# Rotary embedding: larger units, a smaller sine table spread by TensorE, and stores moved between queues

## The chip, the cores and the metric

The kernel runs on one core of a Trainium2 chip. The metric is the device time of one execution in microseconds (us). Seven executions of the kernel before had a median of 85.37 us, from 85.22 to 85.55. The profile comes from one execution and shows five engines (TensorE as PE, VectorE as DVE, ScalarE as ACT, GpSimd as POOL, SyncE as SP) and the 16 DMA engines, which carry the transfers of all queues.

## The reference

The input x has 8 batches of 8 heads, 1024 positions and 64 columns in float32, 16.8 MB. Each position is scaled by 0.5 and multiplied with 32 frequencies; the two halves of the 64 columns are then rotated by that angle.

```python
half = x.shape[-1] // 2
angles = np.outer(positions * scale, freqs)          # 1024 x 32
cos, sin = np.cos(angles), np.sin(angles)
x_first, x_second = x[..., :half], x[..., half:]
out_first = x_first * cos - x_second * sin
out_second = x_first * sin + x_second * cos
out = np.concatenate([out_first, out_second], axis=-1)
```

All 64 heads use the same table of 1024 x 32 sines and cosines. The output is as large as the input.

## The kernel before

The 64 heads are cut into 8 units of 8 heads (L40 to L44). A unit is 2 MB of float32; partition p holds 64 successive positions of one head, so its row is 4096 numbers, 16 KB in memory, and every unit needs the same table of 64 positions x 32 frequencies per partition, because the 16 partitions of a head repeat for each of the 8 heads.

**Loads.** Unit 0 comes in as float32 through SyncE's queue into X0f (L61) and is cast to fp16 by ScalarE (L127). Units 1 to 7 are loaded by GpSimd (L71), whose transfers cast from float32 to fp16 on the way. Each unit has a tile of its own, X0 to X7, so no load waits for anything, and all seven are issued in the first microseconds. Positions and frequencies come in through ScalarE's queue (L64, L66), in this order.

**Table.** The positions lie on 16 partitions, 64 to each. A matmul with a selecting matrix of zeros and ones (sel, made on GpSimd at L76 and L77) repeats them on all 128 partitions (pos_ps, L100). A second one multiplies the frequencies by scale/2pi on every partition (cfreq, L92). VectorE forms the product y (L107), rounds it (m, L114), takes the remainder r (L116) and its absolute value ra (L122), all for 128 x 2048. ScalarE turns r into sinT (L120) and ra into cosT (L126), both fp16.

**Units.** A loop in the order 1, 0, 2, ... 7 (L133) does four VectorE instructions for a unit: ps = X sin (L135), X = X cos (L136), the first half less the product of the second (L137), and the sum for the second half (L140). ScalarE casts the result to float32 into OUT (L144), and SyncE stores it (L145). OUT has 4 buffers, ps has 2.

**Order.** The kernel's author fixes the order on VectorE and ScalarE by hand: `pin` keeps instructions in the order of the program on their engine. Between the engines only the data sets the order: a load ahead of its unit, a cast ahead of its store, and a free buffer ahead of a cast into OUT.

Of the kernel before, what the change touches and what calls it, by code (L numbers as in the profile page):

```python
# [1 line left out]

# [1 line left out]

# [4 lines left out]

FP32 = mybir.dt.float32
FP16 = mybir.dt.float16
I32 = mybir.dt.int32
AF = mybir.ActivationFunctionType
ALU = mybir.AluOpType

_MAGIC = 12582912.0
_TWO_PI_DN = float(np.float32(np.uint32(0x40C90FDA).view(np.float32)))

BUF_O = 4  # L20
BUF_P = 2


@with_exitstack
def kernel(
    ctx: ExitStack,
    tc: tile.TileContext,
    x: bass.AP,
    freqs: bass.AP,
    positions: bass.AP,  # L30
    scale: bass.AP,
    out: bass.AP,
):
    nc = tc.nc

    B, Hh, S, D = x.shape
    NBH = B * Hh
    half = D // 2
    P = nc.NUM_PARTITIONS
    HEADS = 8  # L40
    HP = P // HEADS
    K = S // HP
    N = K * D
    NU = NBH // HEADS  # L44
    assert S % HP == 0 and D == 2 * half and NBH % HEADS == 0

    fscale = float(scale)

    xv = x.rearrange("b h s d -> (b h s d)").rearrange("(u p n) -> u p n", p=P, n=N)
    ov = out.rearrange("b h s d -> (b h s d)").rearrange("(u p n) -> u p n", p=P, n=N)  # L50

    consts = ctx.enter_context(tc.tile_pool(name="consts", bufs=1))
    tmp = ctx.enter_context(tc.tile_pool(name="tmp", bufs=1))
    psum = ctx.enter_context(tc.tile_pool(name="psum", bufs=1, space=bass.MemoryType.PSUM))
    xin = ctx.enter_context(tc.tile_pool(name="xin", bufs=1))
    xout = ctx.enter_context(tc.tile_pool(name="xout", bufs=BUF_O))
    prods = ctx.enter_context(tc.tile_pool(name="prods", bufs=BUF_P))


    X0f = xin.tile([P, N], FP32, name="X0f")  # L60
    nc.sync.dma_start(out=X0f, in_=xv[0])  # L61

    pos_i64 = consts.tile([HP, K], positions.dtype)
    nc.scalar.dma_start(out=pos_i64, in_=positions.rearrange("(q k) -> q k", k=K))  # L64
    freq_row = consts.tile([1, half], FP32)
    nc.scalar.dma_start(out=freq_row, in_=freqs[None, :])  # L66

    X = [xin.tile([P, K, 2, half], FP16, name=f"X{u}") for u in range(NU)]

    def load(u):  # L70
        nc.gpsimd.dma_start(out=X[u].rearrange("p k h j -> p (k h j)"), in_=xv[u])  # L71


    sel = consts.tile([HP, HEADS, HP], FP32)
    load(1)
    nc.gpsimd.memset(sel, 0.0)  # L76
    nc.gpsimd.affine_select(  # L77
        out=sel, in_=sel, compare_op=ALU.not_equal, fill=1.0, base=0,
        pattern=[[0, HEADS], [-1, HP]], channel_multiplier=1,
    )  # L80
    for u in range(2, NU):
        load(u)

    pin = tc.keep_in_program_order


    coef = consts.tile([1, P], FP32)
    pin(nc.vector.memset(coef, fscale / (2.0 * np.pi)))  # L88
    quarter = consts.tile([P, 1], FP32)
    pin(nc.vector.memset(quarter, np.pi / 2.0))  # L90
    cfreq = psum.tile([P, half], FP32)
    nc.tensor.matmul(out=cfreq, lhsT=coef, rhs=freq_row, start=True, stop=True)  # L92

    pos_row = consts.tile([HP, K], FP32)
    pin(nc.vector.tensor_copy(  # L95
        out=pos_row,
        in_=pos_i64.bitcast(I32).rearrange("p (k t) -> p k t", t=2)[:, :, 0],
    ))
    pos_ps = psum.tile([P, K], FP32)
    nc.tensor.matmul(  # L100
        out=pos_ps, lhsT=sel.rearrange("q a b -> q (a b)"), rhs=pos_row, start=True, stop=True
    )
    posf = consts.tile([P, K], FP32)
    pin(nc.vector.tensor_copy(out=posf, in_=pos_ps))  # L104

    y = tmp.tile([P, K, half], FP32)
    pin(nc.vector.tensor_tensor(  # L107
        out=y,
        in0=posf.unsqueeze(2).broadcast_to((P, K, half)),
        in1=cfreq.unsqueeze(1).broadcast_to((P, K, half)),  # L110
        op=ALU.mult,
    ))
    m = tmp.tile([P, K, half], FP32)
    pin(nc.vector.tensor_scalar(out=m, in0=y, scalar1=_MAGIC, scalar2=None, op0=ALU.add))  # L114
    r = tmp.tile([P, K, half], FP32)
    pin(nc.vector.scalar_tensor_tensor(  # L116
        out=r, in0=m, scalar=_MAGIC, in1=y, op0=ALU.subtract, op1=ALU.subtract
    ))
    sinT = consts.tile([P, K, half], FP16)
    pin(nc.scalar.activation(out=sinT, in_=r, func=AF.Sin, bias=0.0, scale=-_TWO_PI_DN))  # L120
    ra = tmp.tile([P, K, half], FP32)
    pin(nc.vector.tensor_scalar(  # L122
        out=ra.bitcast(I32), in0=r.bitcast(I32), scalar1=0x7FFFFFFF, scalar2=None, op0=ALU.bitwise_and
    ))
    cosT = consts.tile([P, K, half], FP16)
    pin(nc.scalar.activation(out=cosT, in_=ra, func=AF.Sin, bias=quarter, scale=-_TWO_PI_DN))  # L126
    pin(nc.scalar.copy(out=X[0].rearrange("p k h j -> p (k h j)"), in_=X0f))  # L127

    cos_b = cosT.unsqueeze(2).broadcast_to((P, K, 2, half))
    sin_b = sinT.unsqueeze(2).broadcast_to((P, K, 2, half))  # L130


    for u in (1, 0, *range(2, NU)):  # L133
        ps = prods.tile([P, K, 2, half], FP16, tag="ps")
        pin(nc.vector.tensor_tensor(out=ps, in0=X[u], in1=sin_b, op=ALU.mult))  # L135
        pin(nc.vector.tensor_tensor(out=X[u], in0=X[u], in1=cos_b, op=ALU.mult))  # L136
        pin(nc.vector.tensor_tensor(  # L137
            out=X[u][:, :, 0, :], in0=X[u][:, :, 0, :], in1=ps[:, :, 1, :], op=ALU.subtract
        ))
        pin(nc.vector.tensor_tensor(  # L140
            out=X[u][:, :, 1, :], in0=ps[:, :, 0, :], in1=X[u][:, :, 1, :], op=ALU.add
        ))
        OUT = xout.tile([P, N], FP32, tag="O")
        pin(nc.scalar.copy(out=OUT, in_=X[u].rearrange("p k h j -> p (k h j)")))  # L144
        nc.sync.dma_start(out=ov[u], in_=OUT)  # L145


# [1 line left out]
_INS = ['x', 'freqs', 'positions', 'scale']  # L149
_OUTS = [((8, 8, 1024, 64), 'float32')]  # L150

_NUMBERS = {'scale': 0.5}


# [26 lines left out]
```

## Time and profile before

| What | Value |
|---|---|
| median of 7 executions | 85.37 us (85.22 to 85.55) |
| the profiled execution | 85.22 us, its span 83.4 us |
| VectorE busy | 62.6 us, 75% of the span, 40 instructions |
| ScalarE busy | 37.4 us, 45%, 12 instructions |
| GpSimd busy | 4.5 us; TensorE 1.1 us |
| HBM read and written | 16.79 and 16.78 MB |

The span runs from the first to the last event that the profile holds; the time of an execution is some 1.8 us longer. The profile gives the busy share of each engine in 40 slices of 2.1 us, with digits for tenths; the shares of the DMA queues, where q1 is SyncE's, q10 ScalarE's and q0 GpSimd's; the chain of work that ended last; and groups of like instructions by line, with their count, busy time, mean duration and the idle time of the engine ahead of them. A window gives, for a stretch of the span, its length, then busy time and count for PE, PE's weight loads, VectorE, ScalarE and GpSimd, then the TensorE clock granted, the DMA share, and the GB/s that arrived. The trace also holds each packet of each DMA queue with its start, duration and size.

### The profile page before, as it was taken

What the parts mean: (1) busy time and instruction counts of PE and PEld (TensorE: products, weight loads), DVE (VectorE), ACT (ScalarE), POOL (GpSimd) and SP (SyncE); (2) the same over time, 40 slices, a digit from 0 to 9 for tenths busy, and PEclk for the clock granted to TensorE, in tenths of its full rate; (3) what the DMA queues carried; (4) which work ended last, traced back from release to release, by engine and by line L of the source; (5) the groups of instructions that cost most, each with busy time, mean ns of one, the idle gap of its engine ahead of it and who ended that gap; (6) DMA issues with size and microseconds to landing.
All of it is one profiled execution on the core that took longest, in us unless ns stands there. A gap on an engine that the chain in (4) does not pass through costs nothing.

```text
span 83.4 us, 151 instructions
## 1 busy us (share of the span) xinstructions
PE 1.1 (1%) x4; PEld 0.9 (1%) x4; DVE 62.6 (75%) x40; ACT 37.4 (45%) x12; POOL 4.5 (5%) x13
## 2 busy tenths in 40 slices
PE   0003100000000000000000000000000000000000
PEld 0004000000000000000000000000000000000000
DVE  0010899699999999999999999999999999600000
ACT  1400000899559129509806912940970691394000
POOL 5960000000000000000000000000000000000000
DMA  5699999999999998999999999999999999999890
GB/s 110 240 342 349 279 200 232 208 224 204 220 220 200 232 177 243 377 302 338 287 318 369 291 330 298 357 463 401 463 408 440 432 416 463 393 471 393 377 503 0
DMA packets 2338, 26.22 MB, mean 314 GB/s; under 512 B 274, under 2 KB 290, under 8 KB 290
## 3 DMA queue, kind: packets, MB, share of 16 engines
q1 hardware_dynamic: 1296, 18.87, 54.2%
q0 software_dynamic: 1008, 7.34, 42.9%
q10 hardware_dynamic: 34, 0.01, 0.1%
HBM read 16.79 MB, written 16.78 MB: 402 GB/s over the span
## 4 chain that ended last, share of the span: by engine, by line
DVE 72%; DMA 7%; ACT 7%; DVEq 1%; PE 1%; issue 1%; ACTq 1%
DVE X L136 22%; DVE ps L135 21%; DVE X L137 12%; DVE X L140 10%; DMA freq_row<-in_freqs_dram 7%; ACT OUT L144 4%; DVE r L116 3%; DVE y L107 3%; ACT sinT L120 2%; DVE m L114 1%; DVEq L176 1%; PE cfreq L92 1%; PE pos_ps L100 1%; ACTq L64 0%; DVE posf L104 0%
## 5 line engine op out<-in xcount | busy, mean ns | idle before, releaser
L144 ACT CAST OUT<-X 128x4096 f32<-128x4096 f16 x8 | 28.8, 3605 | 25.0 <-DVE X L140 25.0
L135 DVE TENSOR_TENSOR ps<-X,sinT 128x4096 f16<-128x4096 f16 x8 | 18.3, 2285 | 0.7 <-ACT sinT L120 0.7
L136 DVE TENSOR_TENSOR X<-X,cosT 128x4096 f16<-128x4096 f16 x8 | 18.3, 2292 | 0.3
L137 DVE TENSOR_TENSOR X<-X,ps 128x2048 f16<-128x2048 f16 x8 | 9.8, 1225 | 0.3
L140 DVE TENSOR_TENSOR X<-ps,X 128x2048 f16<-128x2048 f16 x8 | 9.7, 1217 | 0.0
L120 ACT ACTIVATE sinT<-r 128x2048 f16<-128x2048 f32 x1 | 1.9, 1910 | 11.8 <-DVE r L116 11.8
L71 POOL DMA_DIRECT2D X<-in_x_dram x7 | 3.9, 567 | 0.8 <-POOLq L162 0.8
L127 ACT CAST X<-X0f 128x4096 f16<-128x4096 f32 x1 | 3.6, 3588 | 0.0
L95 DVE CAST pos_row<-pos_i 16x64 f32<-16x64 int32 x1 | 0.3, 272 | 3.8 <-DMA pos_i<-in_positions_dram 3.8
L104 DVE COPY posf<-pos_ps 128x64 f32<-128x64 f32 x1 | 0.2, 225 | 3.5 <-PE pos_ps L100 3.5
L116 DVE SCALAR_TENSOR_TENSOR r<-m,y 128x2048 f32<-128x2048 f32 x1 | 2.3, 2293 | 0.0
L107 DVE TENSOR_TENSOR y<-posf,cfreq 128x2048 f32<-128x2048 f32 x1 | 2.3, 2287 | 0.0
L120 ACT ACT_TABLE_LOAD x1 | 1.3, 1283 | 1.7 <-issue 1.7
L126 ACT ACTIVATE cosT<-ra,quarter 128x2048 f16<-128x2048 f32 x1 | 2.0, 1985 | 0.0
L114 DVE TENSOR_SCALAR m<-y 128x2048 f32<-128x2048 f32 x1 | 1.2, 1226 | 0.0
L122 DVE TENSOR_SCALAR ra<-r 128x2048 int32<-128x2048 int32 x1 | 1.2, 1226 | 0.0
L88 DVE MEMSET coef<- 1x128 f32 x1 | 0.2, 165 | 0.8 <-PEq L162 0.8
L92 PE MATMUL cfreq<-freq_row,coef 1*128 1x32 f32 x2 | 0.6, 391 | 7.5 <-DMA freq_row<-in_freqs_dram 7.5
L100 PE MATMUL pos_ps<-pos_row,sel 16*128 16x64 f32 x2 | 0.7, 432 | 0.0
L92 PEld LDWEIGHTS cfreq<-freq_row,coef 1*128 1x128 f32 x2 | 0.5, 304 | 7.5 <-issue 7.5
L100 PEld LDWEIGHTS pos_ps<-pos_row,sel 16*128 16x128 f32 x2 | 0.5, 328 | 0.0
L77 POOL TENSOR_SCALAR_AFFINE_SELECT sel<-sel 16x128 f32<-16x128 f32 x1 | 0.3, 333 | 0.1
(6 smaller groups left out, 0.7 us busy)
## 6 DMA issues: line engine op xcount, KB each, us to landing
out_dram<-OUT SPq DMA_DIRECT2D x8, 2048.0 KB, 14.5
X<-in_x_dram POOLq DMA_DIRECT2D x7, 1024.0 KB, 24.4
X0f<-in_x_dram SPq DMA_DIRECT2D x1, 2048.0 KB, 10.2
pos_i<-in_positions_dram ACTq DMA_DIRECT2D x1, 8.0 KB, 4.1
freq_row<-in_freqs_dram ACTq DMA_DIRECT2D x1, 0.1 KB
```

What stands on the lines that cost most here:

```text
L71: nc.gpsimd.dma_start(out=X[u].rearrange("p k h j -> p (k h j)"), in_=xv[u])
L100: nc.tensor.matmul(out=pos_ps, lhsT=sel.rearrange("q a b -> q (a b)"), rhs=pos_row, start=True, stop=True)
L107: pin(nc.vector.tensor_tensor(out=y, in0=posf.unsqueeze(2).broadcast_to((P, K, half)), in1=cfreq.unsqueeze(1).broadcast_to((P, K, half)), ...
L114: pin(nc.vector.tensor_scalar(out=m, in0=y, scalar1=_MAGIC, scalar2=None, op0=ALU.add))
L116: pin(nc.vector.scalar_tensor_tensor(out=r, in0=m, scalar=_MAGIC, in1=y, op0=ALU.subtract, op1=ALU.subtract))
L120: pin(nc.scalar.activation(out=sinT, in_=r, func=AF.Sin, bias=0.0, scale=-_TWO_PI_DN))
L127: pin(nc.scalar.copy(out=X[0].rearrange("p k h j -> p (k h j)"), in_=X0f))
L135: pin(nc.vector.tensor_tensor(out=ps, in0=X[u], in1=sin_b, op=ALU.mult))
L136: pin(nc.vector.tensor_tensor(out=X[u], in0=X[u], in1=cos_b, op=ALU.mult))
L137: pin(nc.vector.tensor_tensor(out=X[u][:, :, 0, :], in0=X[u][:, :, 0, :], in1=ps[:, :, 1, :], op=ALU.subtract))
L140: pin(nc.vector.tensor_tensor(out=X[u][:, :, 1, :], in0=ps[:, :, 0, :], in1=X[u][:, :, 1, :], op=ALU.add))
L144: pin(nc.scalar.copy(out=OUT, in_=X[u].rearrange("p k h j -> p (k h j)")))
```

## The change

The units become twice as large: 4 units of 16 heads, 4 MB each. Partition p holds 128 successive positions of a head, so the row of a unit is 8192 numbers, 32 KB in memory. The computation of a unit is done in two halves of 4096 numbers per partition, with the same four VectorE instructions and one ScalarE cast for each half as before for a unit. The loop runs in the order 0 to 3.

Loads: the second half of unit 0 comes in as float32 in two quarters, one through SyncE and one through ScalarE, the latter behind positions and frequencies; the two land in a buffer of OUT's pool. GpSimd loads the first half of unit 0 and the whole of units 1 to 3. On GpSimd, the memset and the select that make sel are now pinned between its loads, and sel has 128 x 2048 elements in fp16 instead of 16 x 128 in float32.

Table: the positions come in on 128 partitions, 8 to each, so that y, m, r, ra and the two Sin instructions have 256 columns. Their results lie in one tile tab. Sixteen fp16 matmuls of 512 columns, each with another slice of sel, copy the rows of tab to where the units need them; six PSUM buffers take the results. Groups 0, 2, 4 and 6 are copied from PSUM into the table T by VectorE, the other twelve by ScalarE, which then casts the second half of unit 0.

Stores: units 0 and 1 are stored whole by GpSimd, after its loads; units 2 and 3 by SyncE, half by half. OUT has 3 buffers of 32 KB per partition, one of which first holds unit 0's two quarters.

```diff
-    HEADS = 8
+    HEADS = 16
...
-    X0f = xin.tile([P, N], FP32, name="X0f")
-    nc.sync.dma_start(out=X0f, in_=xv[0])
-    pos_i64 = consts.tile([HP, K], positions.dtype)
-    nc.scalar.dma_start(out=pos_i64, in_=positions.rearrange("(q k) -> q k", k=K))
+    X0f = xout.tile([P, N], FP32, tag="O")
+    Q = NH // 2
+    pin(nc.sync.dma_start(out=X0f[:, :Q], in_=xv[0][:, NH : NH + Q]))
+    pos_i64 = consts.tile([P, K8], positions.dtype)
+    pin(nc.scalar.dma_start(out=pos_i64, in_=positions.rearrange("(p k) -> p k", k=K8)))
     freq_row = consts.tile([1, half], FP32)
-    nc.scalar.dma_start(out=freq_row, in_=freqs[None, :])
+    pin(nc.scalar.dma_start(out=freq_row, in_=freqs[None, :]))
+    pin(nc.scalar.dma_start(out=X0f[:, Q:NH], in_=xv[0][:, NH + Q :]))
...
+    sel = consts.tile([P, G, HEADS, HP], FP16)
+    pin(nc.gpsimd.dma_start(out=Xf[0][:, :NH], in_=xv[0][:, :NH]))
+    pin(nc.gpsimd.memset(sel, 0.0))
+    pin(nc.gpsimd.dma_start(out=Xf[1], in_=xv[1]))
+    pin(nc.gpsimd.affine_select(
         out=sel, in_=sel, compare_op=ALU.not_equal, fill=1.0, base=0,
-        pattern=[[0, HEADS], [-1, HP]], channel_multiplier=1,
-    )
+        pattern=[[-1, G], [0, HEADS], [-G, HP]], channel_multiplier=1,
+    ))
     for u in range(2, NU):
-        load(u)
+        pin(nc.gpsimd.dma_start(out=Xf[u], in_=xv[u]))
...
+    T = consts.tile([P, 2, K, half], FP16)
+    for g in range(G):
+        ps = spread.tile([P, 2, K8, half], FP32, tag="g")
+        nc.tensor.matmul(
+            out=ps.rearrange("p t k j -> p (t k j)"),
+            lhsT=sel[:, g].rearrange("s h q -> s (h q)"),
+            rhs=tab.rearrange("s t k j -> s (t k j)"),
+            start=True, stop=True,
+        )
+        dst = T[:, :, g * K8 : (g + 1) * K8, :]
+        if g % 2 == 0 and g < G // 2:
+            pin(nc.vector.tensor_copy(out=dst, in_=ps))
+        else:
+            pin(nc.scalar.copy(out=dst, in_=ps))
+    pin(nc.scalar.copy(out=Xf[0][:, NH:], in_=X0f[:, :NH]))
...
-    for u in (1, 0, *range(2, NU)):
+    for u in range(NU):
+        OUT = xout.tile([P, N], FP32, tag="O")
+        for s in range(2):
+            ks = slice(s * KH, (s + 1) * KH)
+            ns = slice(s * NH, (s + 1) * NH)
...
+            pin(nc.scalar.copy(out=OUT[:, ns], in_=Xf[u][:, ns]))
+            if u >= NU // 2:
+                pin(nc.sync.dma_start(out=ov[u][:, ns], in_=OUT[:, ns]))
+        if u < NU // 2:
+            pin(nc.gpsimd.dma_start(out=ov[u], in_=OUT))
```

Here KH is half of K (64), NH half of N (4096), K8 is 8 positions per partition, and G is 16 groups.

## The prediction

> **What bounds the kernel now.** I read the slices of the page first, then its queues, then windows of 5 us.
>
> ```profile
> DVE  0010899699999999999999999999999999600000
> ...
> DMA  5699999999999998999999999999999999999890
> ...
> q1 hardware_dynamic: 1296, 18.87, 54.2%
> q0 software_dynamic: 1008, 7.34, 42.9%
> ...
> HBM read 16.79 MB, written 16.78 MB: 402 GB/s over the span
> ```
>
> ```profile
> 10.00:15.00 5.00, 0.00 (x0) 0.00 (x0) 4.90 (x4) 0.19 (x1) 0.00 (x0) 1.00 1.03 215
> 40.00:45.00 5.00, 0.00 (x0) 0.00 (x0) 4.97 (x4) 1.68 (x2) 0.00 (x0) 1.00 1.01 316
> 60.00:65.00 5.00, 0.00 (x0) 0.00 (x0) 4.93 (x4) 2.14 (x1) 0.00 (x0) 1.00 0.99 423
> ```
>
> The DMA share is the seventh number of the windows, after the clock, and it is 1.0 in all three stages: loads alone, loads and stores mixed, stores alone. The GB/s beside it count what arrives: a load turns float32 into fp16, so 215 arriving is 430 read, 316 is half of each, and 423 is stores. The transfers thus run at one rate from end to end, and the two queues' shares sum to 97.1% of 83.4 us. VectorE is as long a job: the chain that ended last is nearly all VectorE.
>
> ```profile
> 1.19 6.21 DMA freq_row<-in_freqs_dram
> ...
> 7.53 0.60 PE cfreq L92 x2
> ...
> 14.81 1.92 ACT sinT L120
> 16.75 2.30 DVE ps L135
> ...
> 71.16 1.15 DVEq L176
> ...
> 72.38 3.60 ACT OUT L144
> ```
>
> freqs lands at 7.40, the tables take 9.35 us more, and 8 units of 6.94 us run from 16.75 to 72.31. The cast of the last unit ends at 75.98. In the trace's packet records the last store's first row starts at 76.85, just as the one before it drains (77.0); its last row ends at 81.9, its completion is there at 82.27, and 1.18 us of ending follow. So **two bounds meet at the end**: the transfers have no gap to give back, and VectorE has none to lose. A gain must make the transfers shorter, and keep VectorE from becoming later.
>
> **The change, transfers.** No byte is saved; the rows are. The packet records give for a row of 16 KB 625 ns on GpSimd's queue (q0), 611 ns for a store alone on q1 (624 beside loads), and 22 and 9 ns for a bare completion of 4 B. A straight line through row and completion puts a row of 32 KB at 1.228 us on q0, 22 ns under two of 16 KB, and one of 8 KB at 0.315. For each of the 16 DMA engines:
> - before: 56 x 0.625 + 8 x 0.62 (X0f) + 28 x 0.624 + 36 x 0.611 + 0.24 of completions = 79.7 us. From the first packet (1.76) to the last row it took 80.16, so 0.46 go to the cold start and to the first store's arrival.
> - after: loads 16 x 0.315 + 8 x 0.625 + 24 x 1.228 = 39.5; stores 16 x 1.228 (q0) + 32 x 0.611 (SyncE's halves) = 39.2; completions and the small rows of positions 0.45; sum 79.2.
>
> That is **-0.5 us**. No row of 32 KB is in the trace. If it costs as much as two, the 40 of them give 0.9 back (+0.4); if the 0.46 vanish because loads and stores no longer mix until the loads are over, it is -1.0. I take -0.5.
>
> **The change, VectorE's start.** Positions now lie 8 to a partition, so the angles are 256 columns instead of 2048. Two lengths of one kind give the fixed part: VectorE 2285 ns at 4096 and 1220 at 2048, so 155 fixed; ScalarE 3605 at 4096 and 1910 at 2048, so 214.
>
> ```profile
> L144 ACT CAST OUT<-X 128x4096 f32<-128x4096 f16 x8 | 28.8, 3605 | 25.0 <-DVE X L140 25.0
> ...
> L107 DVE TENSOR_TENSOR y<-posf,cfreq 128x2048 f32<-128x2048 f32 x1 | 2.3, 2287 | 0.0
> ```
>
> Count from F, the landing of freqs (7.40 before). cfreq with its issue 0.74; y 0.42; m 0.29; r 0.42; gaps 0.1; sin 0.43; cos 0.5: cos ends at F+2.9. The pos_ps matmul and its copy fall away, and ra lies beside sin. Then 16 selecting matmuls of 512 columns and 16 copies out of PSUM. No such matmul is in the trace: L92 (32 columns, float32) took 391 ns and L100 (64) 432, so 0.39 to 1.0 us. The Trainium skill (TensorE: Matmul & The Clock Gate, Back-to-back issue gap) has columns/1.2 ns while the array is cold, 0.43 each, near the lower end, and I use that. A copy of 512 is 0.64 on ScalarE and 0.69 on VectorE. The eighth group is in place at F+2.9+0.6+7x0.43+0.64 = F+7.15: the first half of unit 0 starts there, 2.2 us sooner after F than now, and ends at F+14.1. But ScalarE has eight more groups (to F+12.25) and then the cast of X0f (3.6, L127), all ahead of its first OUT. The second half can start only at **F+15.9**, a hole of 1.8 us on VectorE. Seven halves of 6.92 follow: VectorE ends at F+64.3. It ended at 72.31, so the chain is even with before at **F = 8.0**, and the 0.5 us of the transfers come out whole if F is at most 7.5.
>
> **When do positions and freqs land?** Everything hangs on this.
>
> ```profile
> pos_i<-in_positions_dram ACTq DMA_DIRECT2D x1, 8.0 KB, 4.1
> ```
>
> Positions were 16 rows, one to a DMA engine; now they are 128 rows of 64 B, eight to an engine, with freqs behind them. In the packet records of before an engine takes one X0f row, its positions row (512 B, 27 ns), one X0f row, the completion (4 B), one X0f row: one packet a turn. freqs is issued by 1.72 and begins only at 5.83, behind the rows already taken in, and its completion comes two 16 KB rows later (7.07). The Trainium skill (DMA: Bandwidth & Descriptors, Queues, rings and completion order) states that a ring is drained by packets of some 9 to 17 descriptors before the engine turns to another. By that rule the 9 descriptors go in one turn, and F stays 7 to 8. By the rows seen here they go one by one: eight turns beside SyncE's 8 KB rows (0.31) and GpSimd's 16 KB rows (0.625) are 8 x 0.94 less what is through before GpSimd's rows arrive, so F = 8.5 to 10.5. For the rule's side: before 3 us only SyncE's short rows compete, and the rows an engine takes in ahead are half as long. I take F = 7.5, estimate 7 to 10.5.
>
> The rest lies under cover. The selecting mask on GpSimd (2048 columns against 128: affine select 333 ns before, some 4 us by columns) is done near 8, needed at F+2.9. ScalarE's quarter of unit 0, behind freqs, takes turns with rows of 32 KB (8 x 1.5 us): it lands near F+12, just when ScalarE gets to it; later costs one for one. OUT has three buffers, the first lent to X0f; the fourth use waits for unit 0's store, over near 52, and is wanted near 63. Unit 1's store is ready at F+40.4 = 47.9 on GpSimd, behind nothing but its loads; the transfers want it when unit 0's store ends, 1.76+0.8+39.5+9.8 = 51.9: 4.0 us of cover. The Trainium skill (SBUF — State Buffer, Summary: rules for kernel authors) warns that descriptors from GpSimd starve while VectorE runs in its faster modes. The trace of before can't show it, as the last load was issued at 5.63, long before the first L135. One L135 is 2.29 us, so a wait for one instruction would still be covered; only a block over several would show. Halved stores on SyncE let the last transfer be 2 MB, as before.
>
> **The rivals.**
> 1. *Transfers bound, 0.5 us shorter* (F up to 7.5): span 82.9. The profiled execution was 85.22 around its span of 83.4, and the median shown is 85.37, so 84.7 by the profile and **84.8** by the median; own range 84.1 to 85.2.
> 2. *The tables come late* (on the other side, decided at F = 8.0): positions go one row a turn. At F = 9.5 VectorE ends 1.5 us later and nothing lies behind it but the last store: 85.37+1.5 = 86.9; F = 8.5 to 10.5 gives 85.9 to 87.9. For it: the alternation seen. Against it: the short rows ahead of it.
> 3. *GpSimd's stores are late*: from its first load's issue at 1.23 to q0's first packet at 5.71 were 4.5 us, about the cover of unit 1's store. Blocked over three or more instructions of VectorE (7 us), the transfers idle 3 us: 88.
> 4. *Nothing changes*: rows of 32 KB cost two of 16 KB, or F lands near 8: 85.2 to 85.5.
>
> **How the numbers follow.** Chances: 50% for the first, 33% for the second, 7% for the third, 10% for the fourth. A measurement of this kernel tells 0.2% (0.17 us) from no change: faster 0.50, same 0.09, slower 0.41. For 8 in 10 the range goes from 84.1, the floor without the 0.46, to 87.7, most of the second rival.
>
> **What will show it.** The landing of freqs, F; the start of the first half (F+7.15) and of the second (F+15.9); the mean of a 32 KB row, 1.23 us; DMA slices full up to the last two. If the slices have a hole before the last store and the chain is VectorE's down to it, rival 2 holds; a hole near 52 means rival 3. I am wrong if F is early and the transfers are still no shorter.

## The result and the profile after

The changed kernel takes 84.92 us in the median (14 runs) against 85.37 us before; the ratio is 0.9942 with a 95% interval of 0.9929 to 0.9954. One further execution took 86.55 us, with a span 1.7 us longer than the others, and is left out. Forecast were 84.8 us and a range of 84.1 to 87.7.

The slices and queues of the changed kernel's page:

```profile
DVE  0029658999899999999999999999999999300000
...
DMA  3899998996997999899989998998999999999991
...
q0 software_dynamic: 864, 15.73, 66.2%
q1 hardware_dynamic: 720, 9.44, 27.4%
...
HBM read 16.79 MB, written 16.78 MB: 406 GB/s over the span
```

VectorE is done 1.3 us sooner than before (at 71.00 instead of 72.31), while the DMA engines are full to the last slice but one. (The 6 and 7 in the middle come from counting rows of 1.2 us in slices of 2.1 us; the packet records show no gap there.) Three windows answer to those of before; behind the fifth busy time stand the granted clock of TensorE (which has no work there, x0, so that its 0.50 costs nothing), the DMA share and the GB/s that arrived:

```profile
35.00:40.00 5.00, 0.00 (x0) 0.00 (x0) 4.93 (x3) 3.61 (x1) 0.00 (x0) 0.50 0.99 210
45.00:50.00 5.00, 0.00 (x0) 0.00 (x0) 4.90 (x5) 1.56 (x2) 0.53 (x1) 0.50 0.97 419
75.00:80.00 5.00, 0.00 (x0) 0.00 (x0) 0.00 (x0) 0.00 (x0) 0.00 (x0) 0.50 0.99 426
```

There is no mixed stage any more: loads to about 42, stores from there on. The chain that ended last, start and duration in us:

```profile
0.74 5.02 DMA pos_i<-in_positions_dram
5.76 0.02 issue
5.78 2.41 DVE posf L98
...
13.17 2.54 ACT T L136 x5
...
18.17 3.50 ACT X L137
21.69 2.30 DVE pr L149
...
69.85 1.15 DVEq L192
71.02 3.60 ACT OUT L157
```

freqs land at 5.9, 1.5 us sooner than before; positions land at 5.76, 0.9 later than before (4.84). Then something unforeseen: posf, a copy of 128x8, takes 2.40 us. The first half of unit 0 starts at 14.28, the second at 21.69, and the last cast starts at 71.02, 1.4 us sooner than before.

Where the time went, from the packet records and SyncE's last instructions of the two profiled executions:

| us | before | after | difference |
|---|---|---|---|
| last row of the last store ends | 81.90 | 81.38 | -0.52 |
| it has landed | 82.25 | 81.73 | -0.52 |
| last landing to the end of the span | 1.19 | 0.89 | -0.30 |
| span | 83.45 | 82.62 | -0.83 |
| time around the span | 1.77 | 2.17 | +0.40 |
| time | 85.22 | 84.79 | -0.43 |

In the mean of all executions the span falls from some 83.65 to 82.72, by 0.9 us, near what the two profiled ones show. The transfers give the half microsecond that was forecast. But there are two more terms, of about the same size and of opposite sign, that the forecast had not at all. The experiments take them one by one.

### The profile page after: what moved, and what is told of

It is laid out like the page before. It is cut to its first block, busy times and chain, and to the rows that moved or that the text cites. A ratio compares the mean times of both kernels' runs of the same rounds, so it can differ in the third digit from the quotient of the medians.

```text
span 82.6 us, 185 instructions
## 1 busy us (share of the span) xinstructions
PE 5.7 (7%) x18; PEld 2.4 (3%) x18; DVE 62.3 (75%) x43; ACT 40.5 (49%) x24; POOL 9.1 (11%) x12
## 4 chain that ended last, share of the span: by engine, by line
DVE 58%; ACT 15%; DMA 6%; issue 5%; PE 3%; DVEq 1%; ACTq 0%
DVE pr L149 20%; DVE X L150 20%; DVE X L154 9%; DMA pos_i<-in_positions_dram 6%; DVE X L151 6%; ACT T L136 6%; ACT OUT L157 4%; ACT X L137 4%; PE ps L126 3%; DVE posf L98 3%; DVEq L192 1%; DVE r L111 1%; DVE y L102 1%; ACT tab L120 1%; ACT tab L115 1%
## 5 line engine op out<-in xcount | busy, mean ns | idle before, releaser
L149 DVE TENSOR_TENSOR pr<-X,T 128x4096 f16<-128x4096 f16 x8 | 18.3, 2292 | 0.8 <-ACT X L137 0.4
L150 DVE TENSOR_TENSOR X<-X,T 128x4096 f16<-128x4096 f16 x8 | 18.3, 2292 | 0.3
L151 DVE TENSOR_TENSOR X<-X,pr 128x2048 f16<-128x2048 f16 x8 | 9.8, 1224 | 0.3
L154 DVE TENSOR_TENSOR X<-pr,X 128x2048 f16<-128x2048 f16 x8 | 9.7, 1218 | 0.0
L136 ACT CAST T<-ps 128x512 f16<-128x512 f32 x12 | 6.2, 627 | 1.6 <-PE ps L126 1.6
L98 DVE CAST posf<-pos_i 128x8 f32<-128x8 int32 x1 | 2.4, 2400 | 4.8 <-DMA pos_i<-in_positions_dram 4.8
L126 PE MATMUL ps<-tab,sel 128*128 128x512 f16 x16 | 5.1, 476 | 4.0 <-ACT tab L120 3.9
L134 DVE CAST T<-ps 128x512 f16<-128x512 f32 x4 | 2.8, 692 | 1.5 <-PE ps L126 1.5
L82 POOL TENSOR_SCALAR_AFFINE_SELECT sel<-sel 128x2048 f16<-128x2048 f16 x1 | 3.9, 3865 | 0.1
L126 PEld LDWEIGHTS <-sel 128*128 128x128 f16 x16 | 1.9, 119 | 6.6 <-issue 3.9
```

The costliest lines, as they stand in the source:

```text
L82: pin(nc.gpsimd.affine_select(out=sel, in_=sel, compare_op=ALU.not_equal, fill=1.0, base=0, pattern=[[-1, G], [0, HEADS], [-G, HP]], chann ...
L98: pin(nc.vector.tensor_copy(out=posf, in_=pos_i64.bitcast(I32).rearrange("p (k t) -> p k t", t=2)[:, :, 0]))
L126: nc.tensor.matmul(out=ps.rearrange("p t k j -> p (t k j)"), lhsT=sel[:, g].rearrange("s h q -> s (h q)"), rhs=tab.rearrange("s t k j -> s ...
L134: pin(nc.vector.tensor_copy(out=dst, in_=ps))
L136: pin(nc.scalar.copy(out=dst, in_=ps))
L149: pin(nc.vector.tensor_tensor(out=pr, in0=Xs, in1=sin_b, op=ALU.mult))
```

## The experiments

**Is the end set by the transfers, and how much may VectorE lose?** Two and four memsets put the VectorE chain back; nothing else changes.

```diff
+    pad = tmp.tile([P, 1024], FP32)
+    for _ in range(2):            # 4 in the second run
+        pin(nc.vector.memset(pad, 0.0))
     y = tmp.tile([P, K8, half], FP32)
```

> Two memsets of 128x1024 float32 on VectorE between posf and y put the whole VectorE chain back by some 2.3 us. Theory (the transfers set the end, and VectorE has some spare): the last store's rows began near 76.5 in the changed kernel, while its cast ended at 74.6 and a store's first row follows a cast by 0.9, so the spare is 1.0 us; the time rises by 2.3 - 1.0 = 1.3 us to 86.2, and the transfers have a gap before the last store. Rival (VectorE's chain sets the end): plus 2.3, 87.2. Rival (the spare is large): no change, 84.9.

> Four such memsets, VectorE 4.6 us later. Theory: 4.6 - 1.0 = 3.6 us, 88.5, that is one for one with the run of two memsets. Rival (VectorE's chain sets the end): 89.5. Rival (large spare): below 87.

Measured: 86.31 us (ratio to before 1.0088, 1.0061 to 1.0114) and 88.41 us (1.034, 1.0305 to 1.0374). The last cast starts 2.31 and 4.68 us later than in the changed kernel (73.33 and 75.70 against 71.02), the time is 1.39 and 3.49 longer. The spans are 1.31 and 3.78 longer (84.03 and 86.50 in the mean, against 82.72). So the spare is 0.9 to 1.0 us, and beyond it VectorE costs one for one in the span; with four memsets the time around the span is 0.3 shorter, which the time shows too. The gap is there in the windows, two of the run with two memsets,

```profile
70.00:75.00 5.00, 0.00 (x0) 0.00 (x0) 3.27 (x3) 1.67 (x1) 0.00 (x0) 0.50 0.98 419
75.00:77.00 2.00, 0.00 (x0) 0.00 (x0) 0.00 (x0) 1.94 (x1) 0.00 (x0) 0.50 0.58 246
```

and the same two of the changed kernel:

```profile
70.00:75.00 5.00, 0.00 (x0) 0.00 (x0) 0.98 (x1) 3.60 (x1) 0.00 (x0) 0.50 1.00 429
75.00:77.00 2.00, 0.00 (x0) 0.00 (x0) 0.00 (x0) 0.00 (x0) 0.00 (x0) 0.50 1.00 426
```

While ScalarE still casts the last half, the DMA engines of the late run drop to 58%.

**VectorE 1.5 us sooner, and the 2.4 us of posf.**

```diff
+    one = consts.tile([P, G, HP], FP16)
...
-    pin(nc.gpsimd.memset(sel, 0.0))
+    pin(nc.gpsimd.memset(one, 0.0))
...
     pin(nc.gpsimd.affine_select(
-        out=sel, in_=sel, ...
-        pattern=[[-1, G], [0, HEADS], [-G, HP]], ...
+        out=one, in_=one, ...
+        pattern=[[-1, G], [-G, HP]], ...
...
+    pin(nc.scalar.copy(out=sel, in_=one.unsqueeze(2).broadcast_to((P, G, HEADS, HP))))
```

> GpSimd makes the selecting matrix for one head only (128 columns in place of 2048) and ScalarE, idle then, copies it out for the 16 heads. Theory on the 2.40 us of posf (VectorE is held while GpSimd's select runs, to 8.15): posf falls to some 0.2 us and y starts near 6.6 instead of 8.29, so VectorE ends 1.7 us sooner; since the transfers set the end, the time stays at 84.9. Rival (posf is slow for a reason of its own): posf stays at 2.4. Rival (VectorE sets the end): 83.2.

Measured: 84.99 us, ratio 0.994 (0.992 to 0.9961), the changed kernel's own. The groups of this run,

```profile
L83 POOL TENSOR_SCALAR_AFFINE_SELECT one<-one 128x128 f16<-128x128 f16 x1 | 0.4, 435 | 0.1
...
L100 DVE CAST posf<-pos_i 128x8 f32<-128x8 int32 x1 | 0.2, 173 | 4.8 <-DMA pos_i<-in_positions_dram 4.8
```

against those of the changed kernel:

```profile
L98 DVE CAST posf<-pos_i 128x8 f32<-128x8 int32 x1 | 2.4, 2400 | 4.8 <-DMA pos_i<-in_positions_dram 4.8
...
L82 POOL TENSOR_SCALAR_AFFINE_SELECT sel<-sel 128x2048 f16<-128x2048 f16 x1 | 3.9, 3865 | 0.1
```

With the select at 0.4 us in place of 3.9, posf takes 173 ns: in the changed kernel VectorE is held until GpSimd's select (4.28 to 8.15) is through. (In the run with SyncE's long rows, further down, in which positions land at 10.7, after a select of the full size is over, posf takes 171 ns: it is the overlap in time that counts.) The last cast starts at 69.50, 1.5 us sooner, and the time does not move. Both readings were right: VectorE is held by the select, and it is off the path at the end.

**None of VectorE's work on the units.** The four instructions of each half are left out, so the result is not the rotation; the tables stay.

> The four VectorE instructions of every half are left out, so the output is x itself; loads, tables, casts and stores stay. Theory (the transfers set the end): no faster than 84.5, with 84.9 as the guess; units are ready as soon as they are loaded, and the stores on SyncE take turns with loads. Rival (VectorE's chain takes part in the end): several us less.

Measured: 84.53 us (0.9895, 0.9875 to 0.9914). The span is 82.72 in the mean of its runs, the same as the changed kernel's 82.72; its 0.4 us lie wholly in the time around the span (1.80 in place of 2.19). VectorE's work on the units thus takes nothing from the span of the changed kernel.

**Are the rows of 32 KB the gain?**

```diff
-    pin(nc.gpsimd.dma_start(out=Xf[1], in_=xv[1]))
+    pin(nc.gpsimd.dma_start(out=Xf[1][:, :NH], in_=xv[1][:, :NH]))
+    pin(nc.gpsimd.dma_start(out=Xf[1][:, NH:], in_=xv[1][:, NH:]))
...
-        pin(nc.gpsimd.dma_start(out=Xf[u], in_=xv[u]))
+        for hs in (slice(0, NH), slice(NH, N)):
+            pin(nc.gpsimd.dma_start(out=Xf[u][:, hs], in_=xv[u][:, hs]))
...
-            pin(nc.gpsimd.dma_start(out=ov[u], in_=OUT))
+            for hs in (slice(0, NH), slice(NH, N)):
+                pin(nc.gpsimd.dma_start(out=ov[u][:, hs], in_=OUT[:, hs]))
```

> Units 1 to 3 are loaded, and units 0 and 1 stored, by two transfers with rows of 16 KB each, on the same queue in the same order. Theory (the gain is the row's fixed cost): 24 rows per DMA engine x (2 x 0.625 - 1.227) = 0.55, 16 x (2 x 0.611 - 1.213) = 0.14 and five completions 0.1: plus 0.8 us, 85.7, more than the whole gain. Rival (the gain comes from the order of loads and stores or the start): 84.9 to 85.0.

Measured: 84.79 us (0.9917, 0.9894 to 0.9941), if anything less than with the long rows. The expectation fails. The rows are as long as said: 1.227 us (load) and 1.213 (store) for 32 KB, 0.625 and 0.611 for 16 KB. But in the packet records a load of 4 MB follows the one before it by 9.685 us with long rows and by 9.735 with short ones: the rows overlap, and 16 KB take 0.6085 us of an engine, not 0.625. The last row ends 0.22 us later than in the changed kernel (81.60 against 81.38), and not 0.8; the time around the span is 1.93 in place of 2.19 and takes that back. Even the 0.22 can't be put down to the rows. With one more load ahead of it on GpSimd the select ends 0.5 us later here, the last cast starts at 71.92 instead of 71.02, and in the packet records the DMA engines wait 0.14 us each, in the mean, for the last store; in the changed kernel they don't wait. And the run with the small select, whose rows are long, ends its last row at 81.60 as well.

**Is the order the gain?** First the changed kernel with all stores on SyncE, so that those of units 0 and 1 run beside loads.

```diff
-            pin(nc.gpsimd.dma_start(out=ov[u], in_=OUT))
+            pin(nc.sync.dma_start(out=ov[u], in_=OUT))
```

> Units 0 and 1 are stored by SyncE as soon as they are cast, so that these stores take turns with the loads of units 2 and 3, rows of 32 KB as before. Theory (row costs alone): 0 to 0.2 us more for rows that take turns (13 ns each, as the packets of the kernel before show), 84.9 to 85.1. Rival (keeping loads and stores apart is the gain): 85.3 or more.

Measured: 85.51 us (1.0009, 0.9994 to 1.0025): the whole gain is gone, and the theory of 84.9 to 85.1 fails. Then the kernel before with the new order of stores alone.

```diff
-        nc.gpsimd.dma_start(out=X[u].rearrange("p k h j -> p (k h j)"), in_=xv[u])
+        pin(nc.gpsimd.dma_start(out=X[u].rearrange("p k h j -> p (k h j)"), in_=xv[u]))
...
-        nc.sync.dma_start(out=ov[u], in_=OUT)
+        pin((nc.gpsimd if u < NU // 2 else nc.sync).dma_start(out=ov[u], in_=OUT))
```

> The kernel before with one part of the change: the stores of the first four units come from GpSimd behind its loads. Theory: its VectorE chain still ends at 72.3, the last store can't begin before 76.85 and takes eight rows, so nothing can come out: 85.2 to 85.5. Rival (the order alone shortens the transfers and the end): 85.0 or less.

GpSimd's memset and select are pinned too, in the order that they had. Measured: 85.06 us (0.9947, 0.9927 to 0.9966): nearly the whole gain is there, without larger units and without a new table. I expected nothing. What both runs share lies for the larger part not in the transfers: the span falls by 0.48 us in the mean, of which the last row of the profiled execution gives 0.21 (81.69). SyncE's instructions at the end show it, start in us, duration in ns, semaphores awaited; the kernel before:

```
82.27 EVENT_SEMAPHORE 28  110, 103     <- the last store lands (110)
82.33 EVENT_SEMAPHORE 28  114, 102
82.39 EVENT_SEMAPHORE 28  115, 101
82.45 EVENT_SEMAPHORE 28  116, 100
82.51 EVENT_SEMAPHORE 28  117, 99
82.57 EVENT_SEMAPHORE 28  118, 111
82.64 DRAIN
```

and the changed kernel:

```
76.90 EVENT_SEMAPHORE 28  117, 112
81.74 EVENT_SEMAPHORE 28  118, 114     <- the last store lands (118)
81.81 DRAIN
```

SyncE checks the semaphores of all transfers, two at a time, the first of each pair in the order of the numbers, some 61 ns a check. Transfers of SyncE and ScalarE take eight numbers in turn. Before, the last store was the eleventh such transfer and got the third number, and five checks follow its landing. In the changed kernel it is the eighth and last in the list, and everything else is checked while it is under way. With all stores on SyncE it is the tenth, number two, with six checks behind it: the end was 1.27 us there, 0.89 in the changed kernel. In the kernel before with the new order of stores the last store is the seventh, no check follows it, and the end is 0.90.

**That alone, in the kernel before:**

```diff
     nc.scalar.dma_start(out=freq_row, in_=freqs[None, :])
+    for i in range(5):
+        spare = consts.tile([1, half], FP32, name=f"spare{i}")
+        nc.sync.dma_start(out=spare, in_=freqs[None, :])
```

> The kernel before, with five small loads of freqs into spare tiles on SyncE behind X0f, so that the last store's semaphore comes last in the list that SyncE checks at the end (in the kernel before it is the third, and 5 checks of 62 ns follow the last landing; in the changed kernel none does). Theory: the end from the last landing to the span's end falls from 1.20 to 0.90 us, the rest stays: 85.37 - 0.31 = 85.1. Rival (the 0.3 us of the end belong to GpSimd's part in the stores): 85.4.

Measured: 85.07 us (0.9966, 0.9952 to 0.998). SyncE's last instructions, as above:

```
77.44 EVENT_SEMAPHORE 28  116, 99
82.38 EVENT_SEMAPHORE 28  117, 111     <- the last store lands (117)
82.45 DRAIN
```

Five useless loads of 128 B make the kernel before 0.29 us faster, and the end is 0.89 us. In GpSimd's part lies none of this. The whole change (84.92 us) is thus some 0.2 us better than these five loads.

**And in the changed kernel with all stores on SyncE.** The six loads were put on SyncE, not on ScalarE as the expectation has it; for the count of semaphores that is the same.

```diff
+    for i in range(6):
+        spare = consts.tile([1, half], FP32, name=f"spare{i}")
+        nc.sync.dma_start(out=spare, in_=freqs[None, :])
...
-            pin(nc.gpsimd.dma_start(out=ov[u], in_=OUT))
+            pin(nc.sync.dma_start(out=ov[u], in_=OUT))
```

> The changed kernel with all stores on SyncE (units 0 and 1 take turns with loads, as in the run before), and six small loads more on ScalarE, so that the last store's semaphore is checked last. Theory (stores beside loads cost the transfers next to nothing; what that run lost was the end, 1.27 against 0.90 us): 85.5 - 0.37 = 85.1, level with the changed kernel within 0.2. Rival (keeping loads and stores apart is worth its loss): 85.4 or more.

Measured: 85.30 us (0.999, 0.9973 to 1.0007), 0.2 below the run without them and 0.4 above the changed kernel. The span is 83.05 in the mean of 12 runs, against 83.32 without the loads and 82.72 for the changed kernel. So the end is worth 0.3 here too, and some 0.3 us remain for stores beside loads. Theory and rival each hold in part. What these 0.3 are stays open. The profiled execution without the loads, the fastest of its twelve, had moved only 0.04 MB less at 80 us than the changed kernel, 0.1 us; the one with them 0.08 MB less, and there the 16 rows that end last do so between 81.01 and 82.00 (81.30 in the mean), in the changed kernel between 80.77 and 81.38 (81.07). So part of it, in that execution, is a single row that ends 0.34 us after all others.

**Do the short rows ahead of positions matter?** SyncE loads the whole second half of unit 0 in rows of 16 KB.

```diff
-    pin(nc.sync.dma_start(out=X0f[:, :Q], in_=xv[0][:, NH : NH + Q]))
+    pin(nc.sync.dma_start(out=X0f[:, :NH], in_=xv[0][:, NH:]))
...
-    pin(nc.scalar.dma_start(out=X0f[:, Q:NH], in_=xv[0][:, NH + Q :]))
```

> SyncE loads the whole second half of unit 0 with rows of 16 KB; ScalarE's quarter falls away. Positions and frequencies are issued as before. Theory (a DMA engine takes one row a queue and turn): the 8 rows of positions now wait 0.62 us each beside SyncE's rows, and land near 8 to 9.5 instead of 5.76; VectorE starts 0 to 1.5 us later, and the time is 84.9 to 85.4. Rival (rows go by packets of 9 to 17 descriptors): positions land at 5 to 6 as now.

Measured: 88.14 us (1.0314, 1.029 to 1.0338), 3.2 us more than the changed kernel. The chain of this run:

```profile
1.17 10.25 DMA freq_row<-in_freqs_dram
11.42 0.14 issue
11.55 0.61 PE cfreq L94 x2
12.17 0.02 issue
12.19 0.43 DVE y L101
```

Positions land at 10.7 and freqs at 11.42; y starts 3.9 us later than in the changed kernel. The direction is the one that was expected, but not the size: expected were a landing at 8 to 9.5, a start later by at most 1.5 us and a time of at most 85.4. One row of a queue a turn it is: in the changed kernel's packets the eight rows of positions stand between SyncE's eight rows of 8 KB (0.31 us each) and are through at 5.26, just as GpSimd's first row begins (4.84). With rows twice as long they are not through by then, and share the rest with both.

**The time around the span.** It is 1.77 or 1.78 us for the kernel before in the mean, each time that it was measured, as in its profile, and 2.19 in the mean of the changed kernel's 14 runs. Twelve or four memsets of one column on VectorE, while it waits for positions:

```diff
+    pad = consts.tile([P, 1], FP32)
+    for _ in range(12):           # 4 in the other run
+        pin(nc.vector.memset(pad, 0.0))
     coef = consts.tile([1, P], FP32)
```

> The changed kernel with four memsets of 128x1 on VectorE while it waits for positions: nothing of the work is later. The time around the span was 2.17 to 2.21 us in all runs with 55 or 56 VectorE instructions in the trace, 1.92 and 1.93 in the two with 58, 1.77 with 48 and 18. Theory (it goes with the length of VectorE's program): with some 59 the span stays at 82.6 and the time falls by 0.25 to 84.65. Rival (it goes with something else in those kernels, such as the number of GpSimd's transfers): 84.9.

> Twelve such memsets, some 67 VectorE instructions. Theory (length of VectorE's program): 84.5 to 84.7, the time around the span 1.75 to 1.95. Rival (something else): 84.9, with 2.2 us around the span.

Measured: 84.79 us (0.9929, 0.9909 to 0.995) and 84.91 us (0.9944, 0.9928 to 0.996). With twelve, the time around falls to 1.77, as the theory said, but the span rises to 83.12 in the mean from 82.72: nothing is won, and the 84.5 to 84.7 expected did not come. With four it is 2.03 in the mean (1.80 to 2.14) at a span of 82.73, and the 0.13 us are within the interval. So this term does depend on the program and not on the work, but what it is stays open; a span alone can't be taken for the time.

## Why the prediction was right, and where it was not

**The transfers bound the end: right.** VectorE 1.5 us sooner or left out leaves the span where it is (82.8 and 82.7 against 82.7), 2.3 us later costs 1.4. In the kernel before VectorE had its share in the end, as the two bounds say: in the packet records its engines wait 0.1 us each, in the mean, for the last store, and the 16 rows that end last do so within 0.14 us of each other; in the changed kernel nothing waits there, and they end within 0.6 us.

**The transfers shorter by 0.5 us: right in size, wrong in cause.** The step that failed is the straight line from rows of 16 KB to rows of 32 KB, with its 22 ns saved per row and 0.5 us in all. The durations held to 1 ns for loads, but durations overlap; by the distance from load to load a long row saves 6 ns, 0.25 us for all 40 of them (an estimate from that distance), and the last rows don't show even that apart from their scatter (81.60 with short rows, 81.38 and 81.60 with long ones). The larger part is the start: by 5 us the changed kernel has read 1.05 MB to 0.93 before, 0.3 us of work at some 430 GB/s, and it keeps that lead. That was not in the sum. SyncE's shorter first rows are not the cause: in the run with SyncE's long rows, 16 KB each, 1.04 MB were read by 5 us as well. What is the cause stays open; no run has it alone. Another 0.1 is the wait for the last store that the kernel before had.

**Left out of the sum:** the end of the kernel (-0.3), counted as fixed at 1.18 us. It depends, as five loads alone show in the kernel before, on which semaphore the last store gets, and that on how many transfers SyncE and ScalarE issue. And the time around the span, taken as 1.82 for both, which grew by 0.4. The two nearly cancel, so that 84.8 came out 0.12 from the truth is in good part luck. (The sum itself, 85.37 - 0.5, gives 84.87.)

**VectorE's start.** The forecast hung on F, the landing of freqs, with an estimate of 7 to 10.5. It was 5.9. Rows of positions did go one a turn, as the packets of before showed, and not by 9 to 17 descriptors, as the Trainium skill (DMA: Bandwidth & Descriptors, Queues, rings and completion order) has it; but GpSimd's rows joined only at 4.84, so the only neighbours were SyncE's short ones. I had seen that relief and given it too little weight. Against it stood a wait that I had not seen: posf was held by the select to 8.18, which puts y at 8.29, as if F were 7.5, the value I had taken. The mask was checked for being ready in time and not for what it holds up. The Trainium skill (SBUF — State Buffer, Who interferes with whom) names casts among the VectorE instructions that may wait for a GpSimd one to end; 2.40 against 0.17 us agrees. From y on, the second half came at +13.4 and not at +15.2, since ScalarE's ten last copies ran in 4.99 us: 0.50 each, where one lasts 0.63 in the mean. Again durations were added that overlap. The matmuls came every 0.43 us, as taken (weight loads at 10.80, 11.22, 11.65 and 12.08). The halves of a unit took 7.04 us each and not 6.92, 0.8 us over seven of them, and VectorE ended at 71.00. ScalarE's quarter of unit 0 landed at 13.1, sooner than the F+12 of the forecast: the rows beside it were the 16 KB ones of unit 0, not rows of 32 KB.

**The second rival** did not come, but is real: in the run with SyncE's long rows positions are late and the kernel takes 88.14 us, past the range. Splitting that load is what keeps the change on the right side. **The third** did not come: unit 1's store was issued in the window of 45 to 50 and the stores run on at 419 GB/s there.

**No change by the order alone**, which I expected of the kernel before, was wrong: it counted VectorE's late end and forgot the checks at the end. VectorE's end did hold back the rest: the DMA engines of that run wait 0.3 us each, in the mean, for the last store.

## What to carry to other kernels

Where a queue is full, take the time of a row from the distance between starts over a long stretch, not from its duration; the same held here for short copies run back to back on ScalarE. Count the end of a kernel as instructions, not as a constant: the last transfer should have the semaphore that is checked last. Small transfers that a chain waits for went one row a turn here, so ask what rows stand beside them, and how long those are.

## What was not expected of the hardware

- A VectorE copy of 128x8 took 2.40 us beside a GpSimd select of 3.87 us and 0.17 us without it.
- Semaphore checks at the end cost some 61 ns each; five of them are 0.3 us of an 85 us kernel.
- 128 rows of 64 B took 5.0 us from issue to landing beside rows of 8 KB, and 9.9 us beside rows of 16 KB.
- The time around the span was 1.77 to 2.22 us in the mean of these kernels, and within some 0.1 us the same in all executions of one kernel, but for the one with four small memsets (1.80 to 2.14); twelve memsets of one column moved 0.4 us from there into the span.
